# Splitting weight slabs into two float32r parts: on the compute engines, or in the transfers

## The chip, the cores and the metric

The kernel runs on one core of one Trainium2 chip. The core has five engines, each with its own in-order queue of instructions: TensorE (PE in the profile, its weight loads PEld), VectorE (DVE), ScalarE (ACT), GpSimd (POOL) and SyncE (SP). Sixteen DMA engines move data between the memory (HBM) and the core's SBUF; a transfer is issued as an instruction in some engine's queue. The metric is the time of the program on the device in microseconds; lower is better.

## The reference

One decoder layer on 512 tokens of width 1024, all in float32:

```
x = x + 1/2 * FFN1(RMSNorm(x))                  # silu(x W_gate) * (x W_up), then W_down; width 2816
x = x + W_out [ConvModule(z); RGLRU(z)],  z = RMSNorm(x) W_in     # W_in 1024 x 2048
x = x + 1/2 * FFN2(RMSNorm(x))
y = RMSNorm(x)
```

The convolution module multiplies two parts of z (one through a sigmoid), runs a causal depthwise convolution of width 31 over the tokens, a LayerNorm over 512 channels and a swish. The recurrent part has a depthwise convolution of width 4, block-diagonal gates, a linear recurrence over the tokens and a GeLU gate.

## The kernel before

**Weights in two parts.** Products are made in float32r, a rounded form of float32. To keep float32's accuracy every operand is split into a high part, its float32r rounding, and a low part, the rest; a product is then three products, high by high, high by low and low by high. Weights come in slabs of 128 x 1024 float32 (512 KB). A slab is used by one *unit* of work: 24 matmuls (8 blocks of 128, three times) for gate, up and mixer products (`mm_feat`, L189), 12 or 24 for down and output products (`mm_tok`, L328).

**The three steps of a slab.** `slab_load` (L113) takes one of three `raw` buffers and issues the load on SyncE. `slab_hi` (L117) takes one of five `hl` buffers, which hold both parts, and has ScalarE cast `raw` into its first half. `slab_lo` (L121) subtracts the high part from `raw` into the second half, on VectorE, or, where the unit is marked `shared` and a running estimate of GpSimd's load allows it, on GpSimd. A `raw` buffer is free again after the subtraction, an `hl` buffer after the last matmul that reads it.

**The order.** The layer is written as a list of units; `run` (L159) goes through it and, ahead of each unit, emits the steps of later slabs: loads five units ahead, high parts three, low parts two (`AHEAD`, L29). Between units it advances the chains of smaller work (norms, LayerNorm, recurrence) and the width-31 convolution, which runs on VectorE as 31 multiply-adds per 128 channels and half of the tokens (L506). A scheduler then sets each engine's final order from these priorities and the tiles' dependences, and puts in the waits.

**The stages.** First-layer gate and up products of ten feature tiles (`w_g1`, `w_u1`), their down products (`w_d1a`), the other twelve tiles and their down products (`w_d1b`) for each half of the tokens; then the mixer's input products (`w_in`), one half of the tokens (256) at a time, so that every slab of `w_in` is loaded twice, the output products (`w_out`), and the second feed-forward part, whose first nine feature tiles are also made for each half of the tokens apart. From `w_d1b` to the last of these a unit works on half of the tokens. A norm (`norm_chain`, L255) takes a sum of squares on ScalarE, two tiny instructions on GpSimd (`ss`, L218 and L221), a scaling on VectorE and transposes on TensorE.

Of the kernel before, what the change touches and what calls it, by code (L numbers as in the profile page):

```python
# [8 lines left out]
F32 = mybir.dt.float32  # L9
F32R = mybir.dt.float32r  # L10
AF = mybir.ActivationFunctionType
ALU = mybir.AluOpType
# [13 lines left out]
RAW_BUFS = 3  # L26
HL_BUFS = 5
ACT_BUFS = 19
AHEAD = (5, 3, 2)  # L29
POOL_CUT = 1  # L30
POOL_AHEAD = 1.0
# [27 lines left out]
def layer_kernel(ctx: ExitStack, tc, x, gains, w_g1, w_u1, w_d1a, w_d1b, w_in,  # L59
# [12 lines left out]
    def nm(s):  # L72
        uid[0] += 1
        return f"{s}_{uid[0]}"
# [37 lines left out]
    # slabs are loaded, then split into two parts of float32r  # L112
    def slab_load(st, src):  # L113
        st["raw"] = wp.tile([P, D], F32, name=nm("raw"), tag="raw", bufs=RAW_BUFS)
        nc.sync.dma_start(st["raw"], src)

    def slab_hi(st):  # L117
        st["hl"] = wp.tile([P, 2, D], F32R, name=nm("hl"), tag="hl", bufs=HL_BUFS)
        S.copy(st["hl"][:, 0, :], st["raw"])  # L119

    def slab_lo(st, shared):  # L121
        eng = V
        if shared:
            clock["pool"] = max(clock["pool"], clock["pe"])
            if clock["pool"] - clock["pe"] < POOL_AHEAD:
                eng = G
                clock["pool"] += 2.4
        if eng is V:
            dve(1.15)
        n = POOL_CUT if eng is G else 1  # L130
        for i in range(n):
            sl = slice(i * D // n, (i + 1) * D // n)
            eng.tensor_sub(st["hl"][:, 1, sl], st["raw"][:, sl],  # L133
                           st["hl"][:, 0, sl].bitcast(F32))
# [24 lines left out]
    def run(units, held):  # L159
# [4 lines left out]
        for i, (src, shared, us, mm, evac) in enumerate(x[:5] for x in units):  # L164
            for stage, ahead in ((0, AHEAD[0]), (1, AHEAD[1]), (2, AHEAD[2])):
                most = HL_BUFS if i < held else len(order)
                while put[stage] < min(nth + ahead + 1, most):
                    q = put[stage]
                    if stage == 0:
                        slab_load(st[q], units[order[q]][0])  # L170
                    elif stage == 1:
                        slab_hi(st[q])
                    else:
                        slab_lo(st[q], units[order[q]][1])
                    put[stage] += 1
            hl = None
            if src is not None:
                hl = st[nth]["hl"]
                nth += 1
            mm(hl)  # L180
            clock["pe"] += us
            if us:
                step_chains()
                step_convs()
            if evac is not None:
                evac()

# [16 lines left out]
    # a bank for the products beside the main ones  # L204
# [137 lines left out]
    # down products of the first group of feature tiles, one half of the  # L342
    # output columns at a time, all tokens
# [23 lines left out]
    # products of two token tiles with the full width of the output  # L367
# [144 lines left out]
    # mean over the channels, the same in every partition  # L512
# [154 lines left out]
    # the same slabs once more, for the other half of the tokens  # L667
# [58 lines left out]
    # last down products and the final norm  # L726
# [103 lines left out]
```

## Time and profile before

| | us |
|---|---|
| median of 2 runs (948.8 to 949.44) | 949.12 |
| profiled execution, span | 945.9 |
| TensorE busy | 907.8 |
| VectorE busy | 475.1 |
| ScalarE busy | 368.6 |
| GpSimd busy | 210.8 |

The span is from the first to the last instruction of the profiled execution; the runs' times are measured apart and hold 3.2 us more. Busy time is the sum of an engine's instructions. Issues of transfers are not counted as busy. In the rows of instruction groups the last number behind the first bar is the mean duration in nanoseconds; behind the second bar stands the idle time of the engine just before such instructions, and what ended it.

### The profile page before, as it was taken

What the parts mean: (1) busy time and instruction counts of PE and PEld (TensorE: products, weight loads), DVE (VectorE), ACT (ScalarE), POOL (GpSimd) and SP (SyncE); (2) the same over time, 40 slices, a digit from 0 to 9 for tenths busy, and PEclk for the clock granted to TensorE, in tenths of its full rate; (3) what the DMA queues carried; (4) which work ended last, traced back from release to release, by engine and by line L of the source; (5) the groups of instructions that cost most, each with busy time, mean ns of one, the idle gap of its engine ahead of it and who ended that gap; (6) DMA issues with size and microseconds to landing.
All of it is one profiled execution on the core that took longest, in us unless ns stands there. A gap on an engine that the chain in (4) does not pass through costs nothing.

```text
span 945.9 us, 11886 instructions
## 1 busy us (share of the span) xinstructions
PE 907.8 (96%) x4796; PEld 776.7 (82%) x4796; DVE 475.1 (50%) x677; ACT 368.6 (39%) x502; POOL 210.8 (22%) x120
## 2 busy tenths in 40 slices
PE   8999999999999999988889798999999999999997
PEld 6988888888888889888878697799988888888885
DVE  6533333333333433989999897555523333333224
ACT  6522221132222334466876554644511222223113
POOL 2000000000000038884856786700000000000001
PEclk9999999999999999998999899999999999999999
DMA  8322222322222344552433444445533222232202
GB/s 273 121 90 99 101 89 93 108 89 89 89 98 103 123 167 149 186 199 99 148 130 119 153 163 150 158 174 181 184 107 111 89 89 89 94 107 89 89 24 89
DMA packets 33401, 115.94 MB, mean 123 GB/s; under 512 B 4673, under 2 KB 4801, under 8 KB 33346
## 3 DMA queue, kind: packets, MB, share of 16 engines
q1 hardware_dynamic: 32770, 114.14, 34.8%
q10 hardware_dynamic: 576, 1.05, 0.3%
q8 instruction: 37, 0.61, 0.3%
q14 instruction: 18, 0.15, 0.0%
HBM read 113.07 MB, written 2.10 MB: 122 GB/s over the span
## 4 chain that ended last, share of the span: by engine, by line
PE 82%; DVE 13%; ACT 1%; DMA 1%; POOL 1%; issue 1%; SPq 0%; POOLq 0%; ACTq 0%; DVEq 0%
PE pgate L194 25%; PE pup L194 24%; PE pd L331 8%; PE pd L329 8%; PE pd L330 8%; PE pz L194 5%; DVE pc L506 4%; DVE xr L462 2%; PE pdl L331 1%; PE pdl L330 1%; PE pdl L329 1%; DVE th L595 1%; DVE xn L226 1%; DVE act L305 1%; DMA raw<-in_w_u 1%
## 5 line engine op out<-in xcount | busy, mean ns | idle before, releaser
L119 ACT CAST hl<-raw 128x1024 fp32r<-128x1024 f32 x208 | 217.7, 1048 | 330.6 <-PE pup L194 149.5
L133 DVE TENSOR_TENSOR hl<-raw,hl 128x1024 fp32r<-128x1024 f32 x136 | 168.2, 1237 | 290.3 <-ACT hl L119 290.3
L133 POOL TENSOR_TENSOR hl<-raw,hl 128x1024 fp32r<-128x1024 f32 x72 | 180.8, 2520 | 390.6 <-ACT hl L119 385.1
L194 PE MATMUL pgate<-h_hi,hl 128*128 128x512 f32 (+1 forms) x880 | 184.6, 352 | 0.8 <-ACT h_hi L246 0.8
L194 PE MATMUL pup<-h_hi,hl 128*128 128x512 f32 (+1 forms) x880 | 184.3, 351 | 0.3 <-DVE sg L303 0.3
L194 PEld LDWEIGHTS pgate<-h_hi,hl 128*128 128x128 f32 x880 | 145.0, 190 | 25.8 <-ACT h_hi L246 1.5
L194 PEld LDWEIGHTS pup<-h_hi,hl 128*128 128x128 f32 x880 | 144.9, 190 | 24.8 <-DVE sg L303 0.5
L329 PE MATMUL pd<-hl,act 128*128 128x512 f32 x304 | 118.4, 390 | 0.0
L331 PE MATMUL pd<-hl,act 128*128 128x512 f32 x304 | 118.3, 389 | 0.0
L330 PE MATMUL pd<-hl,act 128*128 128x512 f32 x304 | 118.3, 389 | 0.0
L506 DVE SCALAR_TENSOR_TENSOR pc<-ub,ch,pc 128x256 f32<-128x256 f32 x232 | 94.6, 477 | 0.0
L194 PE MATMUL pgate<-h_lo,hl 128*128 128x512 f32 (+1 forms) x440 | 92.3, 352 | 1.8 <-DVE h_lo L252 1.8
L194 PE MATMUL pup<-h_lo,hl 128*128 128x512 f32 (+1 forms) x440 | 91.7, 350 | 0.0
L289 ACT ACTIVATE sg<-pgate 128x512 f32<-128x512 f32 (+1 forms) x55 | 28.2, 513 | 159.0 <-PE pgate L194 159.0
L194 PEld LDWEIGHTS pgate<-h_lo,hl 128*128 128x128 f32 x440 | 72.5, 190 | 14.2 <-DVE h_lo L252 2.0
L194 PEld LDWEIGHTS pup<-h_lo,hl 128*128 128x128 f32 x440 | 72.1, 188 | 12.1
L303 DVE TENSOR_TENSOR sg<-pup,sg 128x512 f32<-128x512 f32 (+1 forms) x55 | 32.0, 583 | 94.6 <-PE pup L194 94.6
L758 POOL TENSOR_SCALAR sf<-sf 128x1 f32<-128x1 f32 x4 | 1.2, 300 | 323.7 <-ACT sqo L755 323.7
L194 PE MATMUL pz<-h_hi,hl 128*128 128x256 f32 x512 | 70.4, 287 | 0.0
L331 PEld LDWEIGHTS pd<-hl,act 128*128 128x128 f32 x304 | 57.1, 188 | 11.9
L329 PEld LDWEIGHTS pd<-hl,act 128*128 128x128 f32 x304 | 57.1, 188 | 11.8
L330 PEld LDWEIGHTS pd<-hl,act 128*128 128x128 f32 x304 | 57.1, 188 | 11.7
(118 smaller groups left out, 759.9 us busy)
## 6 DMA issues: line engine op xcount, KB each, us to landing
raw<-in_w_g SPq DMA_DIRECT2D x53, 512.0 KB, 3.2
raw<-in_w_u SPq DMA_DIRECT2D x53, 512.0 KB, 3.2
raw<-in_w_in SPq DMA_DIRECT2D x32, 512.0 KB, 3.2
raw<-in_w_d1b SPq DMA_DIRECT2D x22, 512.0 KB, 3.2
raw<-in_w_out SPq DMA_DIRECT2D x16, 512.0 KB, 3.2
raw<-in_w_d2b SPq DMA_DIRECT2D x12, 512.0 KB, 3.2
raw<-in_w_d1a SPq DMA_DIRECT2D x10, 512.0 KB, 3.2
raw<-in_w_d2a SPq DMA_DIRECT2D x10, 512.0 KB, 3.2
```

The costliest lines, as they stand in the source:

```text
L119: S.copy(st["hl"][:, 0, :], st["raw"])
L133: eng.tensor_sub(st["hl"][:, 1, sl], st["raw"][:, sl], st["hl"][:, 0, sl].bitcast(F32))
L194: PE.matmul(ps, w[:, a, k, :], h[:, k, t0:t0 + n], start=(s == 0 and k == 0), stop=(s == 2 and k == KT - 1))
L226: V.scalar_tensor_tensor(out=xn, in0=xt[t], scalar=ss[:, 1:2], in1=g, op0=ALU.mult, op1=ALU.mult)
L289: S.activation(sg[:, :n], pg[:, :n], AF.Silu)
L303: V.tensor_mul(sg[:, :n], pu[:, :n], sg[:, :n])
L305: V.tensor_sub(act[:, 1, t0:t0 + n], sg[:, :n], act[:, 0, t0:t0 + n].bitcast(F32))
L329: PE.matmul(ps, ahi, whi, start=first, stop=False)
L330: PE.matmul(ps, ahi, wlo, start=False, stop=False)
L331: PE.matmul(ps, alo, whi, start=False, stop=last)
L462: V.scalar_tensor_tensor(out=xr[:, c, :], in0=rxb[:, c, half * HT + k:half * HT + k + HT], scalar=par(c, P_LW + k), in1=xr[:, c, :], op0=A ...
L506: V.scalar_tensor_tensor(out=cv[:, c, :] if j == 30 else acc, in0=src, scalar=par(c, P_DW + j), in1=acc, op0=ALU.mult, op1=ALU.add)
```

## The change

The `raw` buffers go, and `hl` has six buffers in place of five. A slab's three steps become:

1. a load from HBM straight into the first half of `hl`, issued by GpSimd, which casts to float32r on the way;
2. ScalarE writes the negative of that high part into the second half;
3. a second load of the same slab from HBM, issued by GpSimd, which adds to what the second half holds.

The second half then holds slab minus high part. No engine subtracts; the rules that shared the subtractions between VectorE and GpSimd go. (The removed comments, which shift line numbers, are left out below. In the changed kernel the load is at L113, the negation at L116, the accumulating load at L119; the norm's `ss` instructions are at L203 and L206.)

```diff
-RAW_BUFS = 3
-HL_BUFS = 5
+HL_BUFS = 6
...
-POOL_CUT = 1
-POOL_AHEAD = 1.0
...
     def slab_load(st, src):
-        st["raw"] = wp.tile([P, D], F32, name=nm("raw"), tag="raw", bufs=RAW_BUFS)
-        nc.sync.dma_start(st["raw"], src)
+        st["hl"] = wp.tile([P, 2, D], F32R, name=nm("hl"), tag="hl", bufs=HL_BUFS)
+        G.dma_start(st["hl"][:, 0, :], src)
 
     def slab_hi(st):
-        st["hl"] = wp.tile([P, 2, D], F32R, name=nm("hl"), tag="hl", bufs=HL_BUFS)
-        S.copy(st["hl"][:, 0, :], st["raw"])
-
-    def slab_lo(st, shared):
-        eng = V
-        if shared:
-            clock["pool"] = max(clock["pool"], clock["pe"])
-            if clock["pool"] - clock["pe"] < POOL_AHEAD:
-                eng = G
-                clock["pool"] += 2.4
-        if eng is V:
-            dve(1.15)
-        n = POOL_CUT if eng is G else 1
-        for i in range(n):
-            sl = slice(i * D // n, (i + 1) * D // n)
-            eng.tensor_sub(st["hl"][:, 1, sl], st["raw"][:, sl],
-                           st["hl"][:, 0, sl].bitcast(F32))
+        S.mul(st["hl"][:, 1, :], st["hl"][:, 0, :].bitcast(F32), -1.0)
+
+    def slab_lo(st, src):
+        G.dma_start(st["hl"][:, 1, :], src, accum_op=ALU.add)
...
-                        slab_lo(st[q], units[order[q]][1])
+                        slab_lo(st[q], units[order[q]][0])
```

How this stands in the queues, at three places. In the rows below, `DMA` is the issue of a transfer, and the waits name what the instruction waits for: an engine, or (DMASW, DMAHW) a transfer.

GpSimd's queue at the start, where it makes the first norms. Before, from the last clearing of a buffer:

```order
L645 MEMSET rxb 128x4x3
L218 TENSOR_SCALAR ss_108<-ss_108 128x1 [waits Activation_49]
L221 TENSOR_TENSOR ss_108<-ss_108,neghalf 128x1 [waits Pool_49]
L218 TENSOR_SCALAR ss_113<-ss_113 128x1 [waits Activation_49]
L221 TENSOR_TENSOR ss_113<-ss_113,neghalf 128x1 [waits Pool_49]
```

And after, where L113 is a slab's first load and L119 its accumulating load:

```order
L630 MEMSET rxb 128x4x3
L203 TENSOR_SCALAR ss_108<-ss_108 128x1 [waits Activation_49]
L113 DMA hl_149<-in_w_g 128x1024
L206 TENSOR_TENSOR ss_108<-ss_108,neghalf 128x1 [waits Pool_49]
L203 TENSOR_SCALAR ss_113<-ss_113 128x1 [waits Activation_49]
L113 DMA hl_151<-in_w_u 128x1024
L206 TENSOR_TENSOR ss_113<-ss_113,neghalf 128x1 [waits Pool_49]
L113 DMA hl_153<-in_w_g 128x1024
L113 DMA hl_155<-in_w_u 128x1024
L113 DMA hl_157<-in_w_g 128x1024
L113 DMA hl_159<-in_w_u 128x1024
L119 DMA hl_149<-in_w_g 128x1024 [waits Activation_49]
```

The first six loads, which stood at the head of SyncE's queue, now stand among the norm's instructions, the first behind one that waits for ScalarE, and the first accumulating load behind all six.

GpSimd's queue in the first gate and up products, on all tokens, where it had nothing to do before; SyncE's queue before, where a load waits for VectorE's subtraction to free a `raw` buffer:

```order
L115 DMA raw_617<-in_w_g 128x1024 [waits DMAHW6_49,DVE_49]
L115 DMA raw_651<-in_w_u 128x1024 [waits DMAHW7_49,DVE_49]
L115 DMA raw_683<-in_w_g 128x1024 [waits DMAHW0_49,DVE_49]
L115 DMA raw_717<-in_w_u 128x1024 [waits DMAHW1_49,DVE_49]
L115 DMA raw_749<-in_w_g 128x1024 [waits DMAHW2_49,DVE_49]
```

And GpSimd's queue after:

```order
L113 DMA hl_541<-in_w_g 128x1024 [waits DMASW0_49,PE_49]
L119 DMA hl_541<-in_w_g 128x1024 [waits DMASW1_49,Activation_49]
L113 DMA hl_574<-in_w_u 128x1024 [waits DMASW2_49,PE_49]
L113 DMA hl_605<-in_w_g 128x1024 [waits DMASW3_49,PE_49]
L119 DMA hl_574<-in_w_u 128x1024 [waits DMASW4_49,Activation_49]
L119 DMA hl_605<-in_w_g 128x1024 [waits DMASW5_49,Activation_49]
L113 DMA hl_638<-in_w_u 128x1024 [waits DMASW6_49,PE_49]
L119 DMA hl_638<-in_w_u 128x1024 [waits DMASW7_49,Activation_49]
L113 DMA hl_669<-in_w_g 128x1024 [waits DMASW0_49,PE_49]
L113 DMA hl_702<-in_w_u 128x1024 [waits DMASW1_49,PE_49]
```

One queue now holds both transfers of a slab. A load waits for TensorE to free an `hl` buffer, an accumulating load for ScalarE's negation, and every third slab (`hl_541`, `hl_638`) has its accumulating load directly behind its own load.

GpSimd's queue in the mixer, where the first half's recurrence (`xr`, L571 before, L556 after) is made. Before, the subtractions stand there:

```order
L133 TENSOR_TENSOR hl_3208<-raw_3121,hl_3208 128x1024 [waits DMAHW2_49,Activation_49]
L133 TENSOR_TENSOR hl_3289<-raw_3206,hl_3289 128x1024 [waits DMAHW4_49,Activation_49]
L571 TENSOR_TENSOR xr_2905<-xr_2905,i_3112 128x1024 [waits DVE_49,PE_49,Activation_49]
L133 TENSOR_TENSOR hl_3323<-raw_3248,hl_3323 128x1024 [waits DMAHW5_49,PE_49,Activation_49]
L133 TENSOR_TENSOR hl_3361<-raw_3287,hl_3361 128x1024 [waits DMAHW6_49,Activation_49]
```

And after:

```order
L113 DMA hl_3112<-in_w_in 128x1024 [waits DMASW5_49,DMASW0_49,PE_49]
L119 DMA hl_2990<-in_w_in 128x1024 [waits Activation_49]
L113 DMA hl_3153<-in_w_in 128x1024 [waits DMASW7_49,DMASW2_49,PE_49]
L119 DMA hl_3029<-in_w_in 128x1024 [waits Activation_49]
L556 TENSOR_TENSOR xr_2817<-xr_2817,i_3020 128x1024 [waits DVE_49,PE_49,Activation_49]
L113 DMA hl_3191<-in_w_in 128x1024 [waits DMASW4_49,DMASW1_49,PE_49]
L119 DMA hl_3071<-in_w_in 128x1024
L113 DMA hl_3227<-in_w_in 128x1024 [waits DMASW6_49,DMASW3_49,PE_49]
```

Here loads and accumulating loads alternate, the accumulating load three slabs behind the load ahead of it, with the recurrence's product between them.

## The prediction

> **What bounds the kernel now.** First the engines' totals, then the same by stage, then the DMA engines, each time asking which wait ends last. The profiled execution spans 945.9 us; the median of the two runs shown is 949.12 us, 3.2 us more, and I add that 3.2 at the end.
>
> ```profile
> span 945.9 us, 11886 instructions
> PE 907.8 (96%) x4796; PEld 776.7 (82%) x4796; DVE 475.1 (50%) x677; ACT 368.6 (39%) x502; POOL 210.8 (22%) x120
> ```
>
> TensorE's idle time is 945.9 - 907.8 = 38 us; the busy time by stage says where it lies. The cuts are the first matmul on a slab, the first product of `w_d1b` (318 us) and the first of `w_d2a` (684 us). The columns after the length are PE, PEld, DVE, ACT, POOL, granted clock, share of the DMA engines, GB/s.
>
> ```profile
> 0.00:12.00 12.00, 7.51 (x20) 4.15 (x20) 4.05 (x7) 7.17 (x11) 3.57 (x16) 1.00 0.81 293
> 12.00:318.00 306.00, 305.75 (x1407) 252.10 (x1408) 113.52 (x144) 89.58 (x116) 2.88 (x4) 1.00 0.30 103
> 318.00:684.00 366.00, 339.41 (x2265) 312.70 (x2264) 271.30 (x431) 206.61 (x289) 200.88 (x92) 0.97 0.45 158
> 684.00:946.00 262.00, 255.14 (x1108) 207.70 (x1107) 86.28 (x97) 65.22 (x87) 3.44 (x8) 0.99 0.26 89
> ```
>
> Before 318 us TensorE has no gap, so nothing can be won there. The middle zone has 366 - 339.4 = 26.6 us of gaps, with VectorE busy 271 us: this is all that the change could win. It is also where slabs are used fastest, as the DMA issues of this zone show (columns: count, KB, us to landing), with, from the chain of waits (start, length), one unit of 24 matmuls on all tokens and one on half of them:
>
> ```profile
> q1 hardware_dynamic: 15739, 57.27, 44.9%
> raw<-in_w_in SPq DMA_DIRECT2D x32, 512.0 KB, 3.2
> raw<-in_w_g SPq DMA_DIRECT2D x19, 512.0 KB, 3.3
> raw<-in_w_u SPq DMA_DIRECT2D x19, 512.0 KB, 3.2
> raw<-in_w_out SPq DMA_DIRECT2D x16, 512.0 KB, 3.2
> raw<-in_w_d1b SPq DMA_DIRECT2D x15, 512.0 KB, 3.2
> raw<-in_w_d2a SPq DMA_DIRECT2D x6, 512.0 KB, 3.2
> ```
>
> ```profile
> 39.18 5.62 PE pgate L194 x24
> ...
> 650.67 2.81 PE pgate L194 x24
> ```
>
> 32+19+19+16+15+6 = 107 slabs in 366 us, one per 3.42 us; outside the zone, one per 5.62 us. The DMA engines are 45% busy here, so one transfer per slab is far from a limit. What counts for this change is the price of a transfer once the engines are full, and the only full stretch is the start:
>
> ```profile
> 2.00:12.00 10.00, 7.51 (x20) 4.15 (x20) 3.88 (x6) 5.89 (x10) 2.13 (x7) 1.00 0.94 343
> ```
>
> 343 GB/s at 94% busy: a pass of 524,288 bytes costs 1.53 us. (The zone gives the same: 0.449 x 366 us for 57.27 MB is 1.50 us per slab.)
>
> **Part 1, what goes.** The subtractions, by group, and then (count, least, median and longest ns, first and last start) in the zone alone, with the norms' scaling `xn`:
>
> ```profile
> L119 ACT CAST hl<-raw 128x1024 fp32r<-128x1024 f32 x208 | 217.7, 1048 | 330.6 <-PE pup L194 149.5
> L133 DVE TENSOR_TENSOR hl<-raw,hl 128x1024 fp32r<-128x1024 f32 x136 | 168.2, 1237 | 290.3 <-ACT hl L119 290.3
> L133 POOL TENSOR_TENSOR hl<-raw,hl 128x1024 fp32r<-128x1024 f32 x72 | 180.8, 2520 | 390.6 <-ACT hl L119 385.1
> ...
> L133 DVE TENSOR_TENSOR hl<-raw,hl x36: 1208/1225/2926, 319.7 to 683.1; 128x1024 fp32r<-128x1024 f32 x36
> ...
> L133 POOL TENSOR_TENSOR hl<-raw,hl x72: 2343/2403/3822, 341.5 to 607.9; 128x1024 fp32r<-128x1024 f32 x72
> ...
> L226 DVE SCALAR_TENSOR_TENSOR xn<-xt,ss,gbc x8: 1284/2322/3418, 352.8 to 614.2; 128x1024 f32<-128x1024 f32 x8
> ```
>
> VectorE loses 136 x 1.237 = 168 us, of which only 36, some 45 us, lie in the zone; the other 100 lay under a gapless TensorE and are worth nothing. GpSimd loses 181 us, all in the zone. VectorE may also run faster: its `xn` takes 1284 to 3418 ns in that zone, slow where GpSimd works beside it. So the whole 26.6 us is within reach, if nothing else comes in its place. ScalarE keeps 208 instructions of the same shape (negation for cast, 1.05 us each): zero.
>
> **Part 2, what comes: passes of the DMA engines.** A slab is now fetched twice. The casting load I price as one pass, 1.53 us, by the plain load it replaces; no casting load is in the trace, and its bounds are one pass and two. The accumulating load must read its destination in SBUF as well as the slab in HBM: no less than one pass (1.53), and as two reads two passes (3.06); more than two if it is worked through in small steps. I take two, since two times 512 KB have to be read by the same engines. A slab then needs three passes, 4.59 us: below 5.62, above 3.42. In the zone, 107 x 4.59 = 491 us of transfers have to fit into 366: **+125 us**. The five slabs loaded ahead when the zone begins would take off 5 x 4.59 = 23 us; I leave that against the gaps that an in-order queue will leave between transfers. VectorE's relief is worth nothing there, its gaps lying under the wait for slabs. The Trainium skill (Collectives: The Full Stack, section "Part 3: Why 7× under link rate") puts it down to two source reads, not to the addition, that a reducing transfer ran 1.93 times slower than a copy; nothing in this trace can show it, and by it the zone would be 107 x 1.53 x 2.93 = 480 us, +114.
>
> **Part 3, GpSimd's queue.** All 416 transfers are issued there, in order, and each accumulating load waits for ScalarE, which waits for the casting load to land. Rows for the pieces:
>
> ```profile
> DMA to landing us min/median/max: 3.0/3.2/7.8
> ...
> 47.72 0.33 SPq L115 DMA_DIRECT2D raw<-in_w_g  x1
> ...
> 409.69 0.57 POOL L221 TENSOR_TENSOR ss<-ss,neghalf 128x1 f32<-128x1 f32 x1
> ```
>
> An issue costs SyncE 0.33 us; GpSimd's is not in the trace. Below stands 0.33, above its own 2.40 us subtraction; I take 0.9, SyncE's 0.33 and GpSimd's smallest work of this kind, 0.57, since it must compute what is to be moved. Where products run on all tokens, the queue repeats load a, load b, add a, add b, load c, add c. (All of it is an estimate from the rows above.) Counted from the moment add b begins to move: add b until 3.06; load c moves until 4.59, lands 1.7 later (3.2 less a pass) at 6.3; negated at 7.35; add c issued at 8.25, moved at 11.3; the next two loads until 14.4, the first landing at 14.6; negated 15.6; its add issued 16.5, moved 19.6; then the next add b. That is 19.6 / 3 = 6.5 us per slab against 5.62. Behind a waiting add stand the loads of later slabs, whose buffers may long be free. For some 90 such slabs 0.9 x 90 = 81, less five slabs' lead (28), is +53; with landings and issues overlapping better than I drew them it is 0. I take **+30**. In the zone the queue runs load k+3, add k, with no such standstill, and two issues (1.8 us) stay under 3.42: nothing beyond the passes. The `ss` instructions of the norms now stand behind loads that wait for TensorE, up to one 2.81 us unit at four places; TensorE is waiting for slabs there, so zero, and up to +11 if it isn't.
>
> **Part 4, the start.**
>
> ```profile
> 1.94 0.43 SPq L115 DMA_DIRECT2D raw<-in_w_g  x1
> ...
> 5.34 0.22 POOL L218 TENSOR_SCALAR ss<-ss 128x1 f32<-128x1 f32 x1 [2.79 <-ACT xn L217]
> ...
> 7.72 0.22 POOL L218 TENSOR_SCALAR ss<-ss 128x1 f32<-128x1 f32 x1 [1.50 <-ACT xn L217]
> ...
> 17.43 1.11 PE L194 MATMUL pgate<-h_hi,hl 128*128 128x256 f32 x8
> ```
>
> The first load was issued at 1.94; now it stands behind the first `ss` (5.6), the second behind the second (7.9), and the first add behind all six loads. Issued at 8.8, five loads take until 8.8 + 5 x 1.53 = 16.5, the first add until 19.6, landing at 21.3; its first reader ran at 17.43. That is 4 us, growing to 5 by the fourth slab; the other token tiles are loaded in the same stretch (two passes, 3 us): **+8**.
>
> **Sum.** 945.9 + 125 + 30 + 8 = 1109 for the profiled execution, 1112 with the 3.2; I say **1110**, 17% slower.
>
> **The rivals.**
> *The add is as cheap as a copy.* Two passes are 3.06 us, under 3.42: the zone's transfers (327 us) fit. The gaps then close, 945.9 - 26.6 + 8 + 3.2 = 930; with half of them left, 944. For it: if the read of SBUF runs beside the read of HBM it costs nothing, and no row forbids that; against it: the same engines have twice the bytes to take in. It decides at an add of 3.42 - 1.53 = 1.9 us.
> *A fourth pass*, by a cast or an add dearer than I take it. 6.12 us per slab is above 5.62 too, so transfers bound everything: 208 x 6.12 = 1273, and some 30 for start and end, 1305; a fifth pass, 1590. Nothing in the trace speaks against it, since no such transfer is there.
> *GpSimd's issues are the bound.* At 2.40 us each, two per slab are 4.8: the zone takes 514 us (+148), and the loop above grows by 6 x 1.5 / 3 = 3 us per slab, to some +250 outside: 1340. At 1.6 us it is about 1200. For it: GpSimd's subtraction stretched from 2343 to 3822 ns beside VectorE, so the two do hold each other up. The Trainium skill (SBUF — State Buffer, section "SBUF: two separate sides") has a rule to that effect: GpSimd can't write a transfer's descriptors while VectorE runs in a mode that takes both ports, 620 ns becoming 3100. Against it here: the rule names copies, casts and tensor-scalar forms, and VectorE's work in the zone is nearly all of other forms.
> That the change doesn't do what it says is excluded by its order: every slab has its load, negation and add.
>
> **How the numbers follow.** Three passes (1000 to 1200): 0.48. Fourth pass: 0.22. GpSimd's issues: 0.12. Cheap add: 0.18, half of it with its gain mostly given back to GpSimd's waits (945 to 965). Within 2%, which is also about what a measurement of this kernel can tell from no change, is 930 to 968: 0.11; faster 0.07; slower 0.82. The forecast's own range is 1000 to 1200. For eight in ten I leave out the fifth pass and beyond (0.11) and the best of the cheap add (0.07): 938 to 1400.
>
> **What would show it.** Right: the zone's DMA share near 0.9 or more, TensorE's gaps there put down to accumulating loads, VectorE nearly idle in the first 300 us. The zone's DMA share times its length, divided by 107, gives the price of a slab: 4.6 us if I am right. Wrong in size: matmul units that no longer follow each other at 5.62 us between 50 and 300 us mean a fourth pass, or GpSimd's issues if the DMA share stays low. Wrong in sign: a DMA share of 0.8 or less in the zone with TensorE gapless. What would make the prediction wrong first is the price of the add, on which 107 slabs hang at 107 us per us.

## The result: 1115 us after, 949 us before

The changed kernel takes 1115.33 us (median of 2 runs, 1113.22 to 1117.44) against 949.12 before: 1.175 times as long, with a 95% interval from 1.172 to 1.178. The forecast was 1110. That the total came so close is partly luck: two of its terms were off by 37 and some 40 us, in opposite directions.

The first rows of the changed kernel's page (busy time, share of the span, instructions) show where the engines' work went.

```profile
span 1111.5 us, 11994 instructions
PE 964.0 (87%) x4796; PEld 801.9 (72%) x4796; DVE 275.1 (25%) x541; ACT 366.6 (33%) x500; POOL 327.0 (29%) x464
```

VectorE fell from 475 to 275 us, as its 168 us of subtractions went and other operations became faster. It bought nothing: TensorE now idles 1111.5 - 964.0 = 147.5 us in place of 38. Its busy time also rose, by 56 us for the same 4796 matmuls, at a lower granted clock. The busy time by stage, with the same three cuts (columns: window and length, PE, PEld, DVE, ACT, POOL, granted clock, share of the DMA engines, GB/s):

```profile
0.00:354.20 354.20, 326.68 (x1429) 264.01 (x1429) 47.71 (x90) 89.33 (x118) 85.39 (x132) 0.96 0.72 172
354.20:808.10 453.90, 370.44 (x2257) 324.18 (x2256) 191.77 (x397) 211.32 (x294) 176.48 (x239) 0.94 1.02 254
808.10:1111.50 303.40, 266.86 (x1114) 213.74 (x1112) 35.67 (x54) 65.92 (x89) 65.18 (x94) 0.94 0.68 161
```

Before, these stages took 318.4, 365.9 and 261.6 us. So the zone from the first `w_d1b` product to the first `w_d2a` product, where slabs are used fastest, grew by 88.0 us, the stage before it by 35.8, the stage after it by 41.8. In the zone the DMA engines are full (1.02 in the mean; the share counts packets in flight, and can pass 1 a little). In the other two they are about a third idle, and yet time is lost there. These are two different limits. The border between them does not lie quite at the cut: in the first 31 us of the zone the DMA engines are at 0.69 and TensorE is busy for 17.4 us only, and from there on they are at 1.04.

```profile
354.20:385.00 30.80, 17.38 (x54) 12.52 (x53) 2.77 (x4) 7.06 (x9) 7.15 (x10) 0.77 0.69 170
385.00:808.10 423.10, 353.06 (x2204) 311.66 (x2204) 189.00 (x393) 204.25 (x285) 169.33 (x229) 0.95 1.04 260
```

The full DMA engines first: two rows of TensorE's waits (waited for, us in total, times, longest) and one of its stalls in the timeline (start, length, and in brackets the idle time before it and what ended it):

```profile
PE pd L315 <- DMA hl<-in_w_d1b: 26.6, 16, 5.8
...
PE pz L179 <- DMA hl<-in_w_in: 17.0, 16, 3.3
```

```profile
609.75 0.80 PE L315 MATMUL pd<-hl,yhi 128*128 128x512 f32 x1 [3.51 <-DMA hl<-in_w_out]
```

L315 is the product that reads the low part: TensorE has the high part already, and waits 3.51 us for the accumulating load. Of the 26.6 us for `w_d1b` half fall into the first 31 us, before the DMA engines are full.

Then the other limit, outside the zone: GpSimd's queue in the timeline, where gate and up products run on all tokens:

```profile
95.98 0.86 POOL L119 DMA_DIRECT2D hl<-in_w_u  x1 [7.93 <-ACT hl L116]
96.54 0.87 POOL L113 DMA_DIRECT2D hl<-in_w_g  x1
97.07 0.89 POOL L113 DMA_DIRECT2D hl<-in_w_u  x1
104.65 0.88 POOL L119 DMA_DIRECT2D hl<-in_w_g  x1 [6.70 <-ACT hl L116]
106.12 0.89 POOL L119 DMA_DIRECT2D hl<-in_w_u  x1 [0.59 <-ACT hl L116]
106.67 0.90 POOL L113 DMA_DIRECT2D hl<-in_w_g  x1
115.28 0.86 POOL L119 DMA_DIRECT2D hl<-in_w_g  x1 [7.72 <-ACT hl L116]
```

Three loads (L113) and three accumulating loads (L119) take 115.28 - 95.98 = 19.3 us: 6.4 us per slab, where TensorE could use one every 5.62. Most of it is the queue standing still, 6.7 and 7.7 us at a time. An accumulating load is at its head, and waits for ScalarE's negation (L116) of a slab whose load was issued only just before. Over all engines that is the largest wait of the kernel:

```profile
POOL hl L119 <- ACT hl L116: 475.9, 102, 9.3
```

The order is the same at the start of the zone: the accumulating loads of its first seven slabs still stand directly behind their own load or one load later. TensorE meets the standstill less in a wait for a slab than by way of ScalarE, whose queue is in order too. There the negation of a slab that has not landed stands ahead of the gate's activation (`sg`, L274), which frees what the next product needs. Two rows of TensorE's waits, all of them outside the zone, and one place in the timelines of ScalarE and TensorE:

```profile
PE pgate L179 <- ACT sg L274: 19.3, 6, 5.7
...
PE pdl L314 <- ACT sg L274: 9.1, 1, 9.1
```

```profile
238.71 1.06 ACT L116 ACTIVATE hl<-hl 128x1024 fp32r<-128x1024 f32 x1 [6.46 <-DMA hl<-in_w_u]
239.68 0.58 ACT L274 ACTIVATE sg<-pgate 128x512 f32<-128x512 f32 x1
...
240.31 3.78 PE L179 MATMUL pgate<-h_hi,hl 128*128 128x512 f32 x8 [5.74 <-ACT sg L274]
```

### The profile page after: what moved, and what is told of

Same layout as the page of the kernel before. It is cut to its first block, busy times and chain, and to the rows that moved or that the text cites. A ratio compares the mean times of both kernels' runs of the same rounds, so it can differ in the third digit from the quotient of the medians.

```text
span 1111.5 us, 11994 instructions
## 1 busy us (share of the span) xinstructions
PE 964.0 (87%) x4796; PEld 801.9 (72%) x4796; DVE 275.1 (25%) x541; ACT 366.6 (33%) x500; POOL 327.0 (29%) x464
## 3 DMA queue, kind: packets, MB, share of 16 engines
q0 software_dynamic: 59904, 218.13, 81.1%
q1 hardware_dynamic: 2818, 5.07, 1.4%
## 4 chain that ended last, share of the span: by engine, by line
issue 45%; DMA 27%; POOL 15%; PE 10%; ACT 1%; DVE 0%; POOLq 0%; ACTq 0%
POOL hl L113 8%; DMA hl<-in_w_in 7%; POOL hl L119 6%; DMA hl<-in_w_g 6%; DMA hl<-in_w_u 6%; DMA hl<-in_w_d1b 3%; DMA hl<-in_w_out 3%; PE pd L315 2%; DMA hl<-in_w_d2b 2%; PE pd L316 2%; PE pgate L179 1%; PE pd L314 1%; PE pup L179 1%; PE pz L179 1%; DMA hl<-in_w_d2a 1%
## 5 line engine op out<-in xcount | busy, mean ns | idle before, releaser
L116 ACT ACTIVATE hl<-hl 128x1024 fp32r<-128x1024 f32 x208 | 220.2, 1059 | 642.3 <-DMA hl<-in_w_u 187.0
L179 PE MATMUL pgate<-h_hi,hl 128*128 128x512 f32 (+1 forms) x880 | 195.4, 365 | 31.9 <-ACT sg L274 19.3
L315 PE MATMUL pd<-hl,act 128*128 128x512 f32 x304 | 128.1, 421 | 42.0 <-DMA hl<-in_w_d1b 26.6
L316 PE MATMUL pd<-hl,act 128*128 128x512 f32 x304 | 124.9, 411 | 0.0
L314 PE MATMUL pd<-hl,act 128*128 128x512 f32 x304 | 121.1, 409 | 0.6 <-DMA hl<-in_w_d2b 0.6
L288 DVE TENSOR_TENSOR sg<-pup,sg 128x512 f32<-128x512 f32 (+1 forms) x55 | 32.2, 585 | 303.4 <-ACT sg L274 214.5
L315 PEld LDWEIGHTS pd<-hl,act 128*128 128x128 f32 x304 | 60.9, 200 | 63.9 <-DMA hl<-in_w_d1b 32.9
L119 POOL DMA_DIRECT2D hl<-in_w_g x53 | 48.9, 922 | 162.2 <-ACT hl L116 158.5
L179 PE MATMUL pz<-h_hi,hl 128*128 128x256 f32 x512 | 75.5, 296 | 21.5 <-DMA hl<-in_w_in 17.0
L119 POOL DMA_DIRECT2D hl<-in_w_u x53 | 47.8, 903 | 155.0 <-ACT hl L116 141.8
L179 PEld LDWEIGHTS pz<-h_hi,hl 128*128 128x128 f32 x512 | 67.6, 197 | 26.4 <-DMA hl<-in_w_in 20.2
L290 DVE TENSOR_TENSOR act<-sg,act 128x512 fp32r<-128x512 f32 (+1 forms) x55 | 32.2, 585 | 208.2 <-ACT act L289 208.2
L320 DVE SCALAR_TENSOR_TENSOR xt<-pd,xt 128x512 f32<-128x512 f32 x36 | 23.9, 689 | 213.7 <-PE pd L316 213.7
L314 PEld LDWEIGHTS pd<-hl,act 128*128 128x128 f32 x304 | 60.7, 200 | 14.5 <-DMA hl<-in_w_d2b 1.0
```

The lines of the kernel that those rows point to most:

```text
L116: S.mul(st["hl"][:, 1, :], st["hl"][:, 0, :].bitcast(F32), -1.0)
L119: G.dma_start(st["hl"][:, 1, :], src, accum_op=ALU.add)
L179: PE.matmul(ps, w[:, a, k, :], h[:, k, t0:t0 + n], start=(s == 0 and k == 0), stop=(s == 2 and k == KT - 1))
L288: V.tensor_mul(sg[:, :n], pu[:, :n], sg[:, :n])
L290: V.tensor_sub(act[:, 1, t0:t0 + n], sg[:, :n], act[:, 0, t0:t0 + n].bitcast(F32))
L314: PE.matmul(ps, ahi, whi, start=first, stop=False)
```

## The experiments

The spans of the stages are all read from profiled executions at the same three cuts (the cuts are the same matmuls in every kernel). The ratio is to the kernel before, run again beside each of them (medians 947.4 to 949.6).

| kernel | until the zone | zone | rest | median us | ratio to before (95%) |
|---|---|---|---|---|---|
| before | 318.4 | 365.9 | 261.6 | 949.12 | |
| changed | 354.2 | 453.9 | 303.4 | 1115.33 | 1.175 (1.172 to 1.178) |
| alternate order | 326.4 | 440.1 | 276.5 | 1044.29 | 1.099 (1.096 to 1.103) |
| plain load on SyncE | 323.9 | 432.3 | 269.0 | 1027.60 | 1.082 (1.080 to 1.084) |
| second load overwrites | 322.1 | 368.2 | 269.0 | 961.02 (one run) | |
| half of the add | 323.0 | 383.8 | 265.9 | 974.99 | 1.030 (1.026 to 1.033) |
| no second load | 322.2 | 340.9 | 266.5 | 931.33 | 0.983 (0.981 to 0.986) |
| casting load alone | 322.7 | 424.6 | 266.7 | 1016.63 | 1.073 (1.071 to 1.076) |
| every second shared slab | 318.5 | 371.8 | 261.7 | 954.36 | 1.005 (1.003 to 1.007) |

### Is it the addition, or only a second transfer?

```diff
     def slab_lo(st, src):
-        G.dma_start(st["hl"][:, 1, :], src, accum_op=ALU.add)
+        G.dma_start(st["hl"][:, 1, :], src)
```

> The second load of a slab only overwrites the low half in place of adding to it; the subtraction is left out, so the products use the whole slab twice. Queues, waits and the number of transfers are those of the changed kernel. Theory (the addition's second read costs the DMA engines a pass of its own): a slab falls from 4.2 us of the engines (0.811 of 1111.5 us over 208) to about 3.0, the zone's 107 slabs need some 325 us, less than TensorE's 339, and the time falls to 930 to 970. Rival A (GpSimd's issues and the order of its queue are what costs): the number of issues and waits is unchanged, the time stays above 1070. Rival B (casting is the dear part, 2.1 us for either transfer): a slab still costs 4.2 us and the time stays at 1100.

It took 961.02 us. GpSimd's queue holds the same instructions in the same order; only the addition is gone, and with it nearly all of the loss: with the same order, the addition is worth 85.7 us in the zone and 66.5 outside it (32.1 ahead of it, 34.4 behind). The zone in this run, and one row of GpSimd's queue in the stretch shown above:

```profile
322.10:690.30 368.20, 342.11 (x2257) 310.40 (x2256) 188.12 (x395) 207.08 (x288) 134.11 (x234) 0.98 0.93 305
```

```profile
105.10 0.53 POOL L113 DMA_DIRECT2D hl<-in_w_d1a  x1 [4.03 <-PE pgate L179]
```

Here a load at the head of the queue waits for TensorE to free a buffer: with a shorter second transfer the queue keeps up with TensorE. So the order costs little by itself (11.1 us outside the zone in this run, beside the kernel before), and much only together with the length of the accumulating load.

0.93 x 368.2 / 107 = 3.20 us for two copies, 1.60 each. So a casting load is one pass (1.53 us was taken). But 0.93 is nearly full, and the zone is no shorter than before although VectorE has 188 us of work in place of 272. This already speaks against the rival "cheap add", which had the gaps close. (One run only; the loss that it does away with, 154 us, is far beyond the few us by which runs of one kernel differ here.)

### What does the order in GpSimd's queue cost?

```diff
     def slab_load(st, src):
         ...
-        G.dma_start(st["hl"][:, 0, :], src)
+        tc.keep_in_program_order(G.dma_start(st["hl"][:, 0, :], src))
...
     def slab_lo(st, src):
-        G.dma_start(st["hl"][:, 1, :], src, accum_op=ALU.add)
+        tc.keep_in_program_order(G.dma_start(st["hl"][:, 1, :], src, accum_op=ALU.add))
```

> The same transfers, but GpSimd's loads and accumulating loads are kept in program order everywhere, so load k+3 and add k alternate also where products run on all tokens; the middle zone's order was so already. Theory (outside the zone the time is lost to the standstills of GpSimd's queue, 6.4 us per slab against 5.62, not to the DMA engines, 4.2): TensorE is gapless again between 50 and 300 us and after the zone, which takes 50 to 70 us off: 1040 to 1065; the zone stays at about 455 us. Rival (the transfers' price is what costs everywhere): 1100 or more.

1044.29 us: 71 us come back with the same transfers, by a change of their order alone. GpSimd's queue in the same stretch:

```profile
98.13 0.54 POOL L113 DMA_DIRECT2D hl<-in_w_g  x1 [4.18 <-PE pgate L179]
98.66 0.91 POOL L119 DMA_DIRECT2D hl<-in_w_u  x1
103.75 0.54 POOL L113 DMA_DIRECT2D hl<-in_w_u  x1 [4.18 <-PE pup L179]
104.28 0.91 POOL L119 DMA_DIRECT2D hl<-in_w_g  x1
```

Each accumulating load is now that of an earlier slab, whose negation is long done. The queue waits for one thing only, TensorE freeing a buffer, and the period is 5.62 us again. The stages:

```profile
0.00:326.40 326.40, 315.24 (x1428) 257.96 (x1429) 49.15 (x92) 96.28 (x124) 87.31 (x135) 0.99 0.89 193
326.40:766.50 440.10, 365.15 (x2257) 317.08 (x2256) 189.73 (x395) 205.65 (x286) 172.99 (x234) 0.97 1.03 257
766.50:1043.00 276.50, 259.37 (x1114) 209.97 (x1112) 35.67 (x54) 67.94 (x90) 66.57 (x95) 0.98 0.83 177
```

Of the 77.6 us lost outside the zone, 54.7 are gone (8.0 and 14.9 stay). The zone shortens by 13.8; it was expected to stay at about 455, since the order there was taken to alternate already, which it does not for the first slabs.

### What does an accumulating load cost beside a plain one?

```diff
+RAW_BUFS = 3
-HL_BUFS = 6
+HL_BUFS = 5
...
     def slab_load(st, src):
-        st["hl"] = wp.tile([P, 2, D], F32R, name=nm("hl"), tag="hl", bufs=HL_BUFS)
-        G.dma_start(st["hl"][:, 0, :], src)
+        st["raw"] = wp.tile([P, D], F32, name=nm("raw"), tag="raw", bufs=RAW_BUFS)
+        nc.sync.dma_start(st["raw"], src)
 
     def slab_hi(st):
-        S.mul(st["hl"][:, 1, :], st["hl"][:, 0, :].bitcast(F32), -1.0)
+        st["hl"] = wp.tile([P, 2, D], F32R, name=nm("hl"), tag="hl", bufs=HL_BUFS)
+        S.copy(st["hl"][:, 0, :], st["raw"])
+        S.mul(st["hl"][:, 1, :], st["raw"], -1.0)
```

> The first load is the plain one of the kernel before, on SyncE into a raw buffer; ScalarE makes the high part and its negative from it (two instructions of 1.05 us per slab); GpSimd issues the accumulating loads alone. Theory (a casting load costs the same pass as a plain one, and outside the zone only GpSimd's queue was in the way): the zone stays within 10 us of 455, outside TensorE is gapless and the start is that of the kernel before: 1030 to 1050. Rival (the casting load is dearer than a plain one, say 2.1 us of the 4.2): the zone shrinks by 107 x 0.6 = 60 us as well, to 980 or less. ScalarE has 430 us of slab work then, 37 of 38 busy tenths nowhere near full.

1027.6 us, 2 below the range given, and far from the rival. The zone was expected within 10 us of 455 and has 432.3, 8 less than in the alternate order; so the cast on the way and six buffers in place of three and five make little difference there. (ScalarE's second instruction brings waits of its own: TensorE waits 10.5 us for its `gl` there.) The two kinds of transfer now have a queue each, so that the page prices them apart (packets, MB, share of the DMA engines' span of 1025.2 us):

```profile
q0 software_dynamic: 29952, 109.07, 57.1%
q1 hardware_dynamic: 32770, 114.14, 34.4%
```

A plain load takes 0.344 x 1025.2 / 218 = 1.62 us (218 for the 114.14 MB in pieces of a slab's size), an accumulating one 0.571 x 1025.2 / 208 = 2.81 us: 1.73 times as much. The Trainium skill (Collectives: The Full Stack, section "Part 3: Why 7× under link rate") has 1.93 for a reducing transfer against a copying one in collectives. The 1.73 here, from HBM into SBUF, is a little less.

### Does it go by bytes?

Alternate order, and the accumulating load on half of the columns:

```diff
-        tc.keep_in_program_order(G.dma_start(st["hl"][:, 1, :], src, accum_op=ALU.add))
+        tc.keep_in_program_order(G.dma_start(st["hl"][:, 1, 0:D // 2], src[:, 0:D // 2],
+                                             accum_op=ALU.add))
```

> Queue in alternate order, and the accumulating load on the first half of the columns only (256 KB); the other half of the low part stays the negative high part. Theory (a transfer costs by its bytes: 1.63 us for the casting load, half of 2.7 us for the add, 3.0 us per slab, below the zone's 3.42): the zone is no longer filled, 360 to 370, the rest as in the run with the alternate order less some of its 15 us, 955 to 968 us. Rival (most of an add's price is there whatever its size, 2.4 us or more for half of it): 4.0 us per slab or more, zone 425 or more, over 1010 us.

974.99 us: neither. The zone and GpSimd's transfers in this run:

```profile
323.00:706.80 383.80, 348.20 (x2266) 313.32 (x2264) 186.17 (x395) 207.22 (x288) 174.68 (x236) 0.97 0.92 223
```

```profile
q0 software_dynamic: 59904, 163.60, 71.3%
```

0.92 x 383.8 / 107 = 3.30 us per slab; less a copy of 1.60, half an add costs 1.70, where a whole one costs 2.7 (worked out below). The number of packets is that of the changed kernel, 59904, for 163.60 MB in place of 218.13: the halved adds move as many packets, each of half the size. That a packet has a price beside its bytes would fit, but was not tested further. My threshold was wrong as well: I compared 3.0 us with the 3.42 at which the kernel before used slabs. The next run shows that the zone could use one every 3.19.

### What is the relief of VectorE and GpSimd worth?

```diff
     def slab_lo(st, src):
-        G.dma_start(st["hl"][:, 1, :], src, accum_op=ALU.add)
+        pass
```

> The accumulating load is left out: the low part of each slab stays the negative high part, and a slab is fetched once. It leaves out the subtraction, and shows what the relief of VectorE and GpSimd is worth when no second transfer stands in its place. Theory (as the prediction said: the whole 26.6 us of gaps in the zone are within reach of that relief, less some 5 us for the start, which stays): zone 340 to 352, 928 to 942 us. Rival (the gaps belong to the convolution's own chain of matmuls, ScalarE and VectorE, which no subtraction lengthens; the run in which the second load overwrites kept a zone of 368 with VectorE relieved in the same way): zone 360 to 368, 948 to 957 us.

931.33 us. The zone:

```profile
322.20:663.10 340.90, 331.85 (x2265) 307.57 (x2264) 185.41 (x395) 208.63 (x288) 76.78 (x128) 0.99 0.56 169
```

340.9 against 365.9: the relief is worth 25.0 us. That is close to the 26.6 that the prediction called within reach, but it is not the same time. TensorE's gaps shrink from 26.6 us to 9.1, by 17.5; the other 7.5 come off its busy time (331.9 us in place of 339.3, at a granted clock of 0.99 in place of 0.97). With no transfer in the way the zone uses 107 slabs at 340.9 / 107 = 3.19 us. Together with the two runs above this makes a ladder, in spans: before 945.9; without subtractions 929.6 (-16.3, of which +3.8 and +4.9 lie in the first and the last stage); a second copy of each slab 959.3 (+29.7); the addition 1043.0 in the alternate order (+83.7), or 1111.5 in the change's order (+68.5 more). The step of 83.7 changes the order as well as the addition; the alternate order only ever made a stage shorter here, so the zone's part of it, 72 us, is not the order's. In the same order the addition costs 152.2.

### The casting load alone

```diff
     def slab_load(st, src):
         st["raw"] = wp.tile([P, D], F32, name=nm("raw"), tag="raw", bufs=RAW_BUFS)
         nc.sync.dma_start(st["raw"], src)
+        st["hl"] = wp.tile([P, 2, D], F32R, name=nm("hl"), tag="hl", bufs=HL_BUFS)
+        G.dma_start(st["hl"][:, 0, :], src)
 
     def slab_hi(st):
-        st["hl"] = wp.tile([P, 2, D], F32R, name=nm("hl"), tag="hl", bufs=HL_BUFS)
-        S.copy(st["hl"][:, 0, :], st["raw"])
+        pass
```

(From the kernel before; the subtractions stay on VectorE and GpSimd.)

> The casting load alone: SyncE loads the slab as before, GpSimd loads it once more with the cast in place of ScalarE's copy, and the subtraction stays where it was before, on VectorE and GpSimd. Theory (two copies cost 1.62 + 1.63 = 3.25 us per slab, just under 3.42, as where the second load overwrites; ScalarE's relief of 1.05 us per slab is worth nothing): zone 366 to 380, 952 to 970 us. Rival (the casting loads and the 72 subtractions hold each other up in GpSimd's one queue, as the loads and adds do in the changed kernel): gaps outside the zone or a zone over 395, over 985 us. Second rival (a casting load straight into the high part saves a step between landing and product, and the zone shortens): below 944 us.

1016.63 us: the theory missed, and the rival holds. The zone, and three rows of GpSimd's queue in it:

```profile
322.70:747.30 424.60, 358.89 (x2266) 322.06 (x2265) 264.77 (x428) 107.72 (x185) 253.77 (x200) 0.94 0.79 265
```

```profile
449.23 5.19 POOL L134 TENSOR_TENSOR hl<-raw,hl 128x1024 fp32r<-128x1024 f32 x2 [0.59 <-DMA hl<-in_w_in]
454.36 1.10 POOL L117 DMA_DIRECT2D hl<-in_w_in  x2
460.54 2.73 POOL L134 TENSOR_TENSOR hl<-raw,hl 128x1024 fp32r<-128x1024 f32 x1 [5.07 <-DMA hl<-in_w_in]
```

The DMA engines are at 0.79 here, below the 0.93 at which two copies per slab left a zone of 368 us; so it is not their load. Two casting loads (L117) stand behind 5.19 us of subtraction (L134), and the next subtraction then waits 5.07 us for one of them to land, at the head of the queue. Small work behind it waits too: the norms' `xn` on VectorE waited 33.7 us for GpSimd's `ss` in the zone, and TensorE for them.

```profile
PE ptr L243 <- DVE xn L227: 23.9, 4, 8.1
PE pd L331 <- POOL hl L134: 12.6, 8, 1.9
```

This is the same fault as in the changed kernel's gate and up products, made of other instructions: on one in-order queue, an instruction that waits for a transfer stands ahead of those that should start the next.

### Can a part of it be kept?

The relief of 25 us is only to be had if the DMA engines have room. The kernel before, with every second of the 76 slabs that are marked for GpSimd split by negation (from `raw`) and accumulating load, the others as before:

```diff
+ACC_PERIOD = 2
...
+        if shared:
+            nshared[0] += 1
+            st["acc"] = nshared[0] % ACC_PERIOD == 0
+            if st["acc"]:
+                S.mul(st["hl"][:, 1, :], st["raw"], -1.0)
+                G.dma_start(st["hl"][:, 1, :], src, accum_op=ALU.add)
 
     def slab_lo(st, shared):
+        if st.get("acc"):
+            return
```

> The kernel before, with every second slab of those whose subtraction GpSimd may share (38 of 76) split by ScalarE's negation and an accumulating load, the other 38 subtracted on GpSimd; plain loads on SyncE throughout. Theory (the accumulating load costs about 2.7 us of the DMA engines, so a share of the slabs fits where all do not): the zone needs 107 x 1.5 + 38 x 2.7 = 263 of 366 us, VectorE loses its subtractions there, and 5 to 25 us of TensorE's 26.6 us of gaps go: 924 to 944. Rival (an accumulating load's latency or GpSimd's queue brings new waits): 949 or more.

954.36 us, a ratio of 1.005 (1.003 to 1.007): no gain, so the theory missed and the rival's time came. The zone, and whom TensorE waited for:

```profile
318.50:690.30 371.80, 343.65 (x2265) 315.83 (x2264) 247.40 (x427) 243.72 (x328) 145.18 (x96) 0.96 0.77 209
```

```profile
PE pd L340 <- ACT uhi L560: 6.7, 2, 5.5
...
PE pm L532 <- DVE ps L527: 3.8, 2, 2.5
PE pz L205 <- ACT rxb L471: 3.6, 1, 3.6
```

VectorE is relieved by 24 us and the DMA engines have room, but ScalarE has 37 us more, and the steps of the convolution and the recurrence (`uhi`, `rxb`) that stand in its queue keep TensorE waiting (`uhi` 6.7 us, 4.2 before; `rxb` 3.6, 1.1 before). That this is all of it is not shown.

Three more versions free GpSimd of subtractions altogether: the 76 slabs go to accumulating loads by halves or thirds, or not at all, and what is left of them to VectorE. To the edit just shown (with a period of 2, of 3, or none) comes this:

```diff
         eng = V
-        if shared:
-            clock["pool"] = max(clock["pool"], clock["pe"])
-            if clock["pool"] - clock["pe"] < POOL_AHEAD:
-                eng = G
-                clock["pool"] += 2.4
```

> The kernel before with GpSimd freed of subtractions: every second one of the 76 shared slabs gets its low part by negation and accumulating load, the other 38 are subtracted on VectorE. Theory (what slows VectorE in the zone is GpSimd subtracting beside it; the run without a second load had VectorE at 185 us there with a zone of 341; 38 + 31 subtractions of 1.22 us add some 84, while the zone's transfers, 107 x 1.53 + 38 x 2.75 = 268 us, leave the DMA engines at 0.8): zone 346 to 358, 930 to 943 us, faster than both kernels. Rival (ScalarE's 38 more negations and its waits for landing hold the convolution up, as in the run that still subtracted the other 38 on GpSimd): zone 364 to 374, 947 to 957 us.

> The same with every third shared slab by negation and accumulating load (25), the other 51 on VectorE. Theory: as above with 16 us more on VectorE and 36 us less on the DMA engines, 930 to 945 us. Rival (VectorE becomes the bound of the stretch in which the convolution runs): over 950 us.

> The kernel before with all 208 subtractions on VectorE and no accumulating load. Theory (76 x 1.22 = 93 us come to VectorE, some 50 go with the slowing by GpSimd; 185 + 107 x 1.22 = 316 us in a zone of 341 leaves it nearly full, and the convolution waits for it): zone 360 to 385, 945 to 972 us. Rival (GpSimd's subtractions cost VectorE as much time as they take from it): below 943 us.

965.75 us (ratio 1.019, 1.014 to 1.023), 966.32 (1.020, 1.016 to 1.023) and 990.14 (1.044, 1.041 to 1.047): all slower than before. All three theories missed: the first two expected a gain, the third at most 972. The first one's rival was too low as well; the second's, over 950, came; the third's, below 943, fell. TensorE's waits, first with a half on accumulating loads, then with everything on VectorE:

```profile
PE pd L335 <- ACT uhi L555: 9.1, 2, 7.3
PE pm L527 <- DVE ps L522: 8.9, 3, 4.2
PE pm L527 <- ACT i L575: 8.0, 1, 8.0
```

```profile
PE pm L527 <- DVE ps L522: 58.1, 4, 34.4
```

With every subtraction on VectorE, the LayerNorm's `ps`, which follows the convolution there, keeps TensorE waiting 58 us: VectorE is then the bound. Nothing tried beats the kernel before, except the one that leaves the subtraction out.

## Why the prediction was right, and where its terms were wrong

| term | predicted | measured |
|---|---|---|
| zone | +125 | +88.0 (+74.2 in the alternate order) |
| GpSimd's queue outside the zone | +30 | about +70, of which the alternate order removes 54.7 |
| start | +8 | about +8 |
| sum, on 945.9 | 1109 | 1111.5 |

**That nothing is won before the zone, and that VectorE's relief is worth nothing under full DMA engines: right.** VectorE lost 200 us of work, and no stage became shorter. The relief by itself is worth 25.0 us of zone in the run without a second load, but only 17.5 of them are gaps: "the whole 26.6 us is within reach" comes near in size, partly for another reason, TensorE's clock. Which of the subtractions held the zone up is not settled, as no run takes away those of one engine and adds nothing elsewhere: moving all of GpSimd's to VectorE makes it worse, and moving half of them to the transfers, with a second pass on ScalarE, wins nothing. Of the runs made, only the one that takes them from both engines at no other cost sets the zone free.

**"I take two [passes]" for the accumulating load, 3.06 us: a little too dear.** By the test that the prediction set, share times length over 107, the zone of the changed kernel gives 1.02 x 453.9 / 107 = 4.33 us per slab, that of the alternate order 1.03 x 440.1 / 107 = 4.24, where 4.59 was taken. Less a copy of 1.60 the add is 2.6 to 2.7 us in a full zone, and 2.8 as its queue's own packets have it. The zone itself lasted 453.9 us where 491 were summed (463 by the test, since the share is 1.02). I had left five slabs' lead "against the gaps that an in-order queue will leave between transfers". There are such gaps, but only in the first 31 us of the zone, where the share is 0.69; "in the zone the queue runs load k+3, add k, with no such standstill" is wrong for these first slabs, and the alternate order wins 13.8 us in the zone. This is the first mis-sized term, by 37 us; the mechanism, an add that costs the DMA engines clearly more than a copy in a full zone, is shown by the run in which the second load overwrites (368 us) beside the two with the addition (440 and 454).

**GpSimd's queue: the loop was right, the sum made of it was not.** 19.6 us per three slabs were worked out, 19.3 measured; the issue that was taken at 0.9 us takes 0.9 in these rows. The step that failed is "with landings and issues overlapping better than I drew them it is 0. I take +30". They did not overlap better, and I took little more than half of what the drawing gave (+53, against the 54.7 that go with the order). That the standstill reaches TensorE by way of ScalarE's activations as well, 28.4 us in all, the prediction did not have. Measured are 77.6 us outside the zone; less the start's 8 that is 70, and the alternate order takes 54.7 of the 77.6 away. The lead that I subtracted is real ahead of the zone, where TensorE's first wait for a slab after the start comes only at 149 us, as its timeline shows.

```profile
149.59 0.50 PE L315 MATMUL pd<-hl,act 128*128 128x512 f32 x1 [0.96 <-DMA hl<-in_w_d1a]
```

The last stage begins behind a zone that leaves no lead, and loses more (41.8 us) over fewer slabs. The alternate order too keeps 14.9 us there, the run with two plain copies 7.4 and the run with one load 4.9; what makes them up was not taken apart.

**The start: right by the alternate order**, where the stage before the zone is 8.0 us longer and no standstill adds to it. In the changed kernel itself the first product of a low part ran at 22.80 in place of 17.43, 5.4 us later, where about 4 was worked out:

```profile
22.80 1.21 PE L179 MATMUL pgate<-h_hi,hl 128*128 128x256 f32 x8 [0.26 <-DMA hl<-in_w_g]
```

**The rivals.** *A fourth pass* is excluded by 4.24 to 4.33 us per slab (it needed 6.12). *GpSimd's issues as the bound* is excluded by the issues, mostly 0.54 to 0.91 us in either order of the queue; here are their rows in the changed kernel (least, median and longest ns), for `w_u`:

```profile
L119 POOL DMA_DIRECT2D hl<-in_w_u x53: 851/883/1553, 16.4 to 997.2; - x53
```

The rule that VectorE may block them (the Trainium skill, SBUF — State Buffer, section "SBUF: two separate sides", a transfer of 620 ns becoming 3100) did not show: no issue of an accumulating load took longer than 1553 ns. As the prediction said, VectorE's work here is nearly all of forms that the rule does not name, so this hardly puts it to the test. *The cheap add* would have decided at 1.9 us, by the prediction; that was wrong too. The run in which the add costs a plain copy has a zone of 368 us, and a total of 961, not 930 to 944: two copies of 3.20 us per slab do not fit under the 3.19 that the zone could then use. The point at which a gain begins lies below one pass.

**What would show it.** The zone's share near 0.9 or more: 1.02. The gaps put down to accumulating loads: L315's wait for `w_d1b`, 26.6 us. VectorE nearly idle in the first 300 us: 47.7 us busy of 354. The units that "no longer follow each other at 5.62 us" came as well, and the prediction read them as a fourth pass or as GpSimd's issues, although its own loop had 6.5 us per slab. They were a third thing, its own loop: issues of 0.9 us, and a queue that stands still between them for a long transfer.

## What to carry to other kernels

A transfer of 512 KB that adds cost the DMA engines some 1.7 plain ones here, so price the second fetch and the addition in the stage where the DMA engines have least room, against the pace at which that stage could run after the change, not at which it runs now. On an in-order queue, an instruction that waits for a transfer just issued stops everything behind it: put at least one slab's work between a load and the step that needs it, and check the order that comes out, since 71 us hung on it here with the same transfers. Look at the other in-order queues too: what waits for the transfer there holds up what stands behind it. And when two terms of a sum are uncertain, check each against its own stage: a total that fits does not say that they do.

## What the runs showed of the hardware

Some of VectorE's operations are slower beside GpSimd's subtractions, by a factor of nearly two in the mean, and others are not. Groups of the kernel before (count, then busy us and mean ns):

```profile
L506 DVE SCALAR_TENSOR_TENSOR pc<-ub,ch,pc 128x256 f32<-128x256 f32 x232 | 94.6, 477 | 0.0
...
L462 DVE SCALAR_TENSOR_TENSOR xr<-rxb,ch,xr 128x256 f32<-128x256 f32 x24 | 21.0, 902 | 0.0
L226 DVE SCALAR_TENSOR_TENSOR xn<-xt,ss,gbc 128x1024 f32<-128x1024 f32 x8 | 18.7, 2340 | 5.6 <-POOL ss L221 5.6
```

And of the version with every subtraction on VectorE, where GpSimd has only the recurrence's and the norms' small work (the lines have moved by six):

```profile
L468 DVE SCALAR_TENSOR_TENSOR xr<-rxb,ch,xr 128x256 f32<-128x256 f32 x24 | 10.7, 478 | 0.0
L232 DVE SCALAR_TENSOR_TENSOR xn<-xt,ss,gbc 128x1024 f32<-128x1024 f32 x8 | 10.3, 1287 | 4.9 <-POOL ss L227 4.9
```

`xr` falls from 902 to 478 ns and `xn` from 2340 to 1287. For `xr` the mean hides two cases: beside GpSimd the median is 472 ns and the longest 2690, so most are not slowed, and some take up to 2.2 us longer, about the length of a subtraction (2.40 us). The convolution's `pc`, the same instruction on tiles of the same size in the same stretch, was at 477 ns beside GpSimd as well, and never above 484. The difference is in where they read: `pc` accumulates in a PSUM bank and reads one operand from SBUF, `xr` and `xn` read two. By the Trainium skill (SBUF — State Buffer, section "SBUF: two separate sides") a VectorE instruction with two inputs in SBUF contends with a GpSimd instruction that reads SBUF, and one with at most one such input doesn't, outside the modes that take both ports. The rows agree: in this kernel an accumulator in PSUM is sheltered.

The lower granted clock goes with TensorE's waits and not with the DMA engines' load. In the version with every subtraction on VectorE the stretch from 420 to 600 us has a clock of 0.87, with TensorE busy for 131.7 of 180 us and the DMA engines at 0.39 (columns as in the windows above); where the second load overwrites, the zone has 0.98, with TensorE busy for 342 of 368 us and the DMA engines at 0.93.

```profile
420.00:600.00 180.00, 131.72 (x948) 122.68 (x947) 152.37 (x268) 108.19 (x152) 12.85 (x8) 0.87 0.39 128
```

In the changed kernel the lower clock goes with the 56 us more of TensorE's busy time. Where slabs set the pace TensorE would wait in that time anyway; what the clock adds of its own was not measured apart.
